# Sums of input tiles for the seven-product scheme, formed on the tensor engine in PSUM instead of on GpSimd

## Chip, cores and metric

The kernel runs on one core of one Trainium2 chip. The metric is the device time of one execution in microseconds. Three runs of the kernel before gave 1523.73, 1523.97 and 1529.43 us, a median of 1523.97 us.

## What is computed

One inference step of two trunk layers over 576 tokens, a prompt of 512 and eight samples of 8, with a model width of 1024. Layer 0 mixes time with RWKV-7 and retention heads side by side, layer 1 with a gated short convolution; a squared-ReLU MLP with 4096 hidden channels follows each mixer, and each step ends in a LayerNorm over the residual. Everything is fp32.

```python
def conv_mixer(x, buf0, w_in, conv_w, w_out):
    bg, cg, h = jnp.split(x @ w_in, 3, axis=-1)
    u = cg * h
    ext = jnp.concatenate([buf0.astype(u.dtype), u], axis=1)
    conv = sum(ext[:, j:j + T] * conv_w[j] for j in range(CONV_W))
    return (bg * conv) @ w_out, ext[:, ext.shape[1] - (CONV_W - 1):]

def sqrelu_mlp(x, w_up, w_down):
    return jnp.square(jax.nn.relu(x @ w_up)) @ w_down
...
        x = layer_norm(ALPHA * x + y, ln1_g[l], ln1_b[l])
        x = layer_norm(ALPHA * x + sqrelu_mlp(x, w_up[l], w_down[l]), ln2_g[l], ln2_b[l])
```

## The kernel before

The first stage, some 480 us, is the mixer of layer 0 and is not touched. The rest, `trunk` from line 1692 on, holds the MLP of layer 0, the convolution layer and the MLP of layer 1.

**Layout.** The activations stand transposed, channels on the 128 partitions and the 576 tokens along the free dimension, as eight tiles `x[0..7]`. Each is worked on in two halves of 288 tokens, g = 0 and g = 1. To keep fp32 accuracy, each operand of a matmul is split in two parts of type fp32r, a high part (the value rounded, a copy on ACT) and a low part (the value less its high part, a subtraction on DVE). `parts` (lines 72 to 79) makes them; in a profile their tiles are named h or l with a letter: wh and wl for weights, he and le, ho and lo for the input, hh and hl for the hidden tiles, ht and lt for the sums below. A product of two split operands is three matmuls (`mm3`, line 150): high by high, high by low, low by high.

**Weights.** Weight tiles of 128 x 1024 come by DMA into raw buffers, and `ensure` splits them ahead of their use (lines 77 and 78). Units in the set `T.pairs` are loaded two at a time, and `prepare` (line 117) forms their sums and differences on POOL and DVE (the helper of line 123).

**Two kinds of product.** `gemm` (line 157) does a plain product: for each output tile and half, 8 k-steps of three matmuls into one of six accumulators acc. `gemm7` (line 185) and `chained7` (line 225) do two output tiles and both halves with seven products of half the depth instead of eight, by Strassen's scheme in Winograd's form: the input is taken as a 2 x 2 block matrix, with even and odd tiles `x[2k]` and `x[2k+1]` and the two halves as its blocks. Three of the seven products take blocks as they are: el, the even tile's first half (`xe`), and both halves ol and or of the odd tile (`xo`). The other four take sums of blocks: er - el, or - (er - el), or - er, and ol - (or - (er - el)), which are kept split in `xt[k]`, n = 0 to 3. `x7` (line 1790) lists what each of the seven products takes: el, ol, then sums 1, 0 and 2, then or, then sum 3.

**Where the sums are formed.** `sums` (line 1720) forms 4 x 4 sums. For each k, four subtractions on GpSimd (POOL in the profile) go from the fp32 tiles x to two wide tiles ts, and then two calls of `split` go from ts to xt. It is called as `after` of three plain products, by line 181: in the MLP of layer 0, whose first product (unit 38) has four plain tiles, after the four tiles' first halves; in the convolution (unit 102, six plain tiles, three of them the head) and in the MLP of layer 1 (unit 134, four plain tiles), after both halves of the head. The second half of the even tiles, er, is stored split in the two upper hidden tiles (`b12`, line 1713).

**LayerNorm.** The last tiles of the product ahead end in `ln0_finish`, `ln_finish` and `ln_end`. They write the input's parts (lines 344, 345, 375, 376), and after them the fp32 tile x (lines 346 and 377), which is the residual. Their sums over channels are matmuls into PSUM tiles cps, ps and pq, from the pool `misc` of two banks (line 1663).

**Order.** Each engine has one queue. The program is built under `TileContext(nc, schedule_with_timeline_sim=True)`, which fixes each engine's order when it is built: among the instructions that an estimated timeline has ready, the one that was written first goes first. So products can be mixed in PE's queue.

The choices that bear on this: `NPL = 4` plain tiles, `SUMV = ()` (none of the sums on DVE), `FAR1, FAR2 = 3, 4` weight tiles of the next product split ahead into the tiles of xt, and these lines:

```python
x7 += [xe, [cut(a, gs[0]) for a in xo]] + [[(a[0][:, n], a[1][:, n]) for a in xt] for n in (1, 0, 2)] + [[cut(a, gs[1]) for a in xo], [(a[0][:, 3], a[1][:, 3]) for a in xt]]
T.gemm(102, 6, xs, evac_in, head=3, after=sums)
```

Of the kernel before, what the change touches and what calls it, by code (L numbers as in the profile page):

```python
# [10 lines left out]
F32 = mybir.dt.float32  # L11
F32R = mybir.dt.float32r
AF = mybir.ActivationFunctionType
ALU = mybir.AluOpType
PSUM = bass.MemoryType.PSUM

P = 128
NT = 576
GN = 288
# [476 lines left out]
def par_off():  # L496
    off, c = {}, 0
    for n, w in PARS:
        off[n] = (c, w)
        c += w  # L500
    return off, c
# [887 lines left out]
SUMV = ()  # L1389
# [114 lines left out]
def build(tc, i, o, coff):  # L1504
    nc = tc.nc
    T = Trunk(tc, i['w'], ahead=2)
    with ExitStack() as es:
        sr, sq = es.enter_context(ExitStack()), ExitStack()

        def pool(n, b, st=es, **k):  # L1510
            return st.enter_context(tc.tile_pool(name=n, bufs=b, **k))
# [5 lines left out]
        with ExitStack() as s1:  # L1517
            M = Mixers(T, i, o, coff)
# [28 lines left out]
            ts = [(M, M1)[k // 4].lr.rearrange('p a b c d -> p (a b c d)')[:, NT * (k % 4):NT * (k % 4 + 1)] for k in range(KT)]  # L1547
# [3 lines left out]
            for k, t in enumerate(ts):  # L1551
                x = nc.scalar.copy(M.xs[k][0], t)
# [106 lines left out]
        with ExitStack() as s2:  # L1659
            T.halves = False  # L1660
            T.cap = 2 * T.nu - 1
            wsp = [pool('wspa', WA, s2)] * WA
            T.pools([pool('raw3', RB, s2)], wsp, pool('acc', 6, s2, space=PSUM), pool('misc', 2, s2, space=PSUM), pool('tmp', 1, s2))
            T.start_at(38)
            T.tb = TB
            T.gated = GATED
            T.chunk, T.kfirst = CH, KF
            T.cfg = CFG
            T.pairs = {u + j for u in (38, 134) for j in range(NPL, 8, 2)} | {u + 16 * q + 2 * j for u in (38, 134) for q in range(1, 4) for j in range(4)} | set(range(108, 126, 2))
            hp = pool('hp', 1, s2)  # L1670
            T.ones1024 = hp.tile([P, P], F32, name='o1'); T.ones128 = hp.tile([P, P], F32, name='o2')
            T.eps = hp.tile([P, 1], F32, name='ep'); nc.gpsimd.memset(T.eps, LN_EPS)
            nc.gpsimd.memset(T.ones1024, 1 / 1024); nc.gpsimd.memset(T.ones128, 1 / 128)
            pre = nc.scalar.preload_act_table_set('natural_log_exp_and_others')
            for a in M.tabled:
                tc.add_manual_dep(pre.ins, a.ins.name, mybir.DependencyInfo(mybir.DependencyClass.NoSync, mybir.DependencyReason.DATA), reason='act table')
            T.pre = pre
            two = lambda n, w, hp=hp: tuple(hp.tile([P] + w, F32R, name=c + n) for c in ('h', 'l'))
            T.xe = [two(f'e{k}', [GN]) for k in range(4)]
            T.xo = [two(f'o{k}', [NT]) for k in range(4)]  # L1680
            T.hs = [(hp.tile([P, NT], F32R, name=f'hh{k}'), hp.tile([P, NT], F32R, name=f'hl{k}')) for k in range(KT)]
            nc.scalar.copy(T.hs[7][0], W.y[7])
            nc.vector.tensor_tensor(out=T.hs[7][1], in0=W.y[7], in1=T.hs[7][0].bitcast(F32), op=ALU.subtract)

            def opened():
                sq.close()
                T.p_w4 = xt = pool('xt', 1, s2)
                T.xt = [two(f't{k}', [4, GN], xt) for k in range(4)]
                if WB: wsp.extend([pool('wspb', WB, s2)] * WB)
            trunk(T, s2, par, i, o, W, opened)  # L1690

def trunk(T, es, par, i, o, W, opened):
    nc, tc, x, hs = T.nc, T.tc, T.x, T.hs
    xe, xo, xt = T.xe, T.xo, []
    pt = T.p_tmp
    po, _ = par_off()
# [4 lines left out]
    gs = [slice(0, GN), slice(GN, NT)]  # L1701
    b3 = lambda a: a.rearrange('p (b t) -> p b t', b=8)
    tmp = lambda n: pt.tile([P, GN], F32, tag='t', name=n, bufs=T.tb)
    cut = lambda pair, s: (pair[0][:, s], pair[1][:, s])
# [5 lines left out]
    def split(dst, src):  # L1710
        T.parts(*dst, src)

    def b12(k):
        return cut(hs[6 + k // 2], gs[k % 2])
# [3 lines left out]
        return cut(xo[k], gs[g]) if m % 2 else b12(k) if g else xe[k]  # L1718

    def sums():  # L1720
        for k in range(4):
            ts = [T.wide('ts').rearrange('p (a b) -> p a b', a=2) for _ in range(2)]
            t = lambda n: ts[n // 2][:, n % 2]
            (el, er), (ol, or_) = [[x[2 * k + j][:, s] for s in gs] for j in range(2)]
            for n, (a, b) in enumerate(((er, el), (or_, t(0)), (or_, er), (ol, t(1)))):
                (nc.vector if n in SUMV else nc.gpsimd).tensor_tensor(out=t(n), in0=a, in1=b, op=ALU.subtract)  # L1726
            for n in range(2): split((xt[k][0][:, 2 * n:2 * n + 2], xt[k][1][:, 2 * n:2 * n + 2]), ts[n])

    def xs(k, g):
        return cut(xo[k // 2], gs[g]) if k % 2 else b12(k // 2) if g else xe[k // 2]  # L1730
# [36 lines left out]
    def mlp(u, ln, out):  # L1767
        for q in range(4):
            n = NPL if q == 0 else 0
            if n: T.gemm(u, n, xs, evac_up, head=4, after=sums)  # L1770
            for j in range(n, 8, 2):
                T.gemm7(u + 16 * q + j, x7, evac_up7(j))
            T.gemm(u + 16 * q + 8, 8, hx, res_evac(T.ln_state(ln, x), lnpar(ln), out, first=q == 0, final=q == 3), tail=TL if q == 3 else 0, far=(FAR1 if ln == 1 else 0) if q == 3 else 0)
# [3 lines left out]
    for g in range(2):  # L1777
        for m, (hi, lo) in enumerate(W.w7):
            a = T.p_acc.tile([P, GN], F32, tag='acc', name='acc')
# [58 lines left out]
    def evac_in7(k0, w):  # L1838
        def f(j, t, a):
# [14 lines left out]
            else:  # L1854
# [4 lines left out]
                split(hs[k], t)  # L1859
        return f  # L1860
    T.gemm(102, 6, xs, evac_in, head=3, after=sums)
    for k in range(2, 8, 2):
        for w in range(3):
# [15 lines left out]
```

## Time and profile before

| | us |
|---|---|
| median of three runs | 1523.97 |
| the profiled execution | 1531.27 |
| its span, first to last instruction | 1529.3 |

The mean granted clock of PE over the span is 0.975. Busy times of a page are sums of durations within one engine. Matmuls are pipelined: the duration of one is longer than the distance between the starts of two, so PE's load is better read from how many matmuls stand in a stretch. The page's slices show PE full nearly throughout:

```profile
PE   8999999999998999999999999999998999999996
PEld 7999898989886989999999989999998999999996
DVE  4656766766857984845748679688799475574755
ACT  5343323333323851523515445444376253351533
POOL 1133213346533421311213547332543131121354
```

```profile
L152 PE MATMUL acc<-hh,wh 128*128 128x288 f32 x1180 | 345.9, 297 | 0.3 <-ACT hh L77 0.3
L152 PE MATMUL acc<-ht,wh 128*128 128x288 f32 x444 | 132.9, 300 | 13.7 <-ACT s L244 5.1
L152 PE MATMUL acc<-lt,wh 128*128 128x288 f32 x444 | 132.0, 298 | 3.8 <-DVE lt L78 3.8
```

A row of the groups reads: line, engine, operation, output <- inputs, shape, count; busy time and the mean of one in ns; idle time of the engine just before the group, and what ended most of it. The second and third row are products that take sums.

### The profile page before, as it was taken

What the parts mean: (1) busy time and instruction counts of PE and PEld (TensorE: products, weight loads), DVE (VectorE), ACT (ScalarE), POOL (GpSimd) and SP (SyncE); (2) the same over time, 40 slices, a digit from 0 to 9 for tenths busy, and PEclk for the clock granted to TensorE, in tenths of its full rate; (3) what the DMA queues carried; (4) which work ended last, traced back from release to release, by engine and by line L of the source; (5) the groups of instructions that cost most, each with busy time, mean ns of one, the idle gap of its engine ahead of it and who ended that gap; (6) DMA issues with size and microseconds to landing.
All of it is one profiled execution on the core that took longest, in us unless ns stands there. A gap on an engine that the chain in (4) does not pass through costs nothing. (4 is left out here: it accounts for less than half of the span.)

```text
span 1529.3 us, 29744 instructions
## 1 busy us (share of the span) xinstructions
PE 1473.3 (96%) x11792; PEld 1424.9 (93%) x11792; DVE 1046.1 (68%) x2019; ACT 646.8 (42%) x1365; POOL 499.5 (33%) x554
## 2 busy tenths in 40 slices
PE   8999999999998999999999999999998999999996
PEld 7999898989886989999999989999998999999996
DVE  4656766766857984845748679688799475574755
ACT  5343323333323851523515445444376253351533
POOL 1133213346533421311213547332543131121354
PEclk9999999999888999999999999999999999999998
DMA  5333334445312041331413402223303223142221
GB/s 182 107 88 89 88 100 135 143 123 172 96 43 106 2 136 57 98 97 57 136 57 98 132 7 69 80 87 121 103 1 125 70 87 107 56 126 68 86 67 63
DMA packets 71196, 140.04 MB, mean 92 GB/s; under 512 B 21488, under 2 KB 30944, under 8 KB 71056
## 3 DMA queue, kind: packets, MB, share of 16 engines
q1 hardware_dynamic: 68544, 130.87, 27.5%
q10 hardware_dynamic: 1440, 3.65, 0.7%
q0 software_dynamic: 1072, 3.61, 0.7%
q8 instruction: 93, 1.52, 0.4%
q14 instruction: 47, 0.39, 0.1%
HBM read 124.39 MB, written 13.70 MB: 90 GB/s over the span
## 5 line engine op out<-in xcount | busy, mean ns | idle before, releaser
L77 ACT CAST wh<-raw 128x512 fp32r<-128x512 f32 x440 | 252.7, 618 | 404.1 <-PE acc L152 269.6
L78 DVE TENSOR_TENSOR wl<-raw,wh 128x512 fp32r<-128x512 f32 x440 | 322.3, 765 | 46.9 <-ACT wh L77 41.2
L152 PE MATMUL acc<-hh,wl 128*128 128x288 f32 x1180 | 348.5, 296 | 0.0
L152 PE MATMUL acc<-hl,wh 128*128 128x288 f32 x1180 | 347.9, 296 | 0.0
L152 PE MATMUL acc<-hh,wh 128*128 128x288 f32 x1180 | 345.9, 297 | 0.3 <-ACT hh L77 0.3
L152 PEld LDWEIGHTS acc<-hl,wh 128*128 128x128 f32 x1180 | 221.5, 188 | 0.5
L152 PEld LDWEIGHTS acc<-hh,wl 128*128 128x128 f32 x1180 | 221.4, 188 | 0.5
L152 PEld LDWEIGHTS acc<-hh,wh 128*128 128x128 f32 x1180 | 220.5, 188 | 0.9 <-ACT hh L77 0.5
L152 PE MATMUL acc<-ht,wh 128*128 128x288 f32 x444 | 132.9, 300 | 13.7 <-ACT s L244 5.1
L152 PE MATMUL acc<-xh,wh 128*128 128x288 f32 x464 | 143.0, 308 | 0.0
L123 POOL TENSOR_TENSOR s<-raw 128x512 f32<-128x512 f32 x37 | 53.2, 1437 | 273.4 <-DMA raw<-in_w 208.2
L152 PE MATMUL acc<-xh,wl 128*128 128x288 f32 x464 | 141.0, 304 | 0.0
L152 PE MATMUL acc<-xl,wh 128*128 128x288 f32 x464 | 140.9, 304 | 0.0
L152 PE MATMUL acc<-lt,wh 128*128 128x288 f32 x444 | 132.0, 298 | 3.8 <-DVE lt L78 3.8
L152 PE MATMUL acc<-ht,wl 128*128 128x288 f32 x444 | 131.3, 298 | 0.0
L123 POOL TENSOR_TENSOR raw<-raw 128x512 f32<-128x512 f32 x37 | 57.4, 1552 | 163.7 <-DVE raw L123 110.7
L152 PE MATMUL acc<-ho,wh 128*128 128x288 f32 x352 | 104.2, 296 | 0.0
L152 PE MATMUL acc<-lo,wh 128*128 128x288 f32 x352 | 104.1, 297 | 0.0
L152 PE MATMUL acc<-ho,wl 128*128 128x288 f32 x352 | 103.5, 297 | 0.0
L152 PEld LDWEIGHTS acc<-ht,wh 128*128 128x128 f32 x444 | 84.8, 191 | 15.5 <-ACT s L244 5.4
L152 PEld LDWEIGHTS acc<-xh,wh 128*128 128x128 f32 x464 | 88.1, 190 | 2.5 <-issue 0.2
L152 PEld LDWEIGHTS acc<-xl,wh 128*128 128x128 f32 x464 | 88.1, 190 | 2.1 <-issue 0.2
(526 smaller groups left out, 3460.9 us busy)
## 6 DMA issues: line engine op xcount, KB each, us to landing
raw<-in_w SPq DMA_DIRECT2D x160, 512.0 KB, 3.9
raw<-in_w SPq DMA_DIRECT2D x60, 256.0 KB, 2.8
la<-in_w SPq DMA_DIRECT2D x32, 128.0 KB, 2.7
A<-stg SPq DMA_DIRECT2D x9, 288.0 KB, 2.3
x<-in_x POOLq DMA_DIRECT2D x8, 288.0 KB, 6.2
out_y<-x SPq DMA_DIRECT2D x16, 144.0 KB, 2.8
kr<-A SPq DMA_DIRECT2D x6, 288.0 KB, 2.7
lr<-in_x ACTq DMA_DIRECT2D x4, 288.0 KB, 7.5
```

The costliest lines, as they stand in the source:

```text
L77: a = self.nc.scalar.copy(hi[:, s], src[:, s])
L78: b = self.nc.vector.tensor_tensor(out=lo[:, s], in0=src[:, s], in1=hi[:, s].bitcast(F32), op=ALU.subtract)
L123: tt = lambda e, o, x, y, op: e.tensor_tensor(out=o, in0=x, in1=y, op=op)
L152: mm = lambda w, x, a, b: self.nc.tensor.matmul(acc, lhsT=w, rhs=x, start=a, stop=b, skip_group_check=onto)
```

## The change

The sums are no longer formed from the fp32 tiles x on GpSimd. PE forms each in a PSUM tile tps of the pool misc: every term is multiplied by plus or minus the identity, its high part and its low part in turn, and all of a sum's matmuls accumulate in one bank. Sum 0 has 2 terms, sum 1 has 3, sum 2 has 2, and sum 3 has 4, so 4, 6, 4 and 8 matmuls; each sum is now formed from input blocks directly rather than from an earlier sum. ACT then copies the bank to the high part, and DVE subtracts that from the bank for the low part, one half tile at a time. Before, ACT and DVE did two sums in one instruction, from SBUF. The places of the call are the same, and so is what xt holds. The two unit matrices, of 512 bytes a partition each, are made on ACT when the stage opens. The wide tiles ts are no longer used.

```diff
@@ -1669,6 +1669,8 @@
             hp = pool('hp', 1, s2)
             T.ones1024 = hp.tile([P, P], F32, name='o1'); T.ones128 = hp.tile([P, P], F32, name='o2')
+            T.unit = [hp.tile([P, P], F32R, name=f'u{n}') for n in range(2)]
+            for n in range(2): nc.scalar.activation(T.unit[n], M.C['ident'], AF.Copy, scale=2.0 * n - 1.0)
             T.eps = hp.tile([P, 1], F32, name='ep'); nc.gpsimd.memset(T.eps, LN_EPS)
@@ -1718,13 +1720,18 @@
     def sums():
+
         for k in range(4):
-            ts = [T.wide('ts').rearrange('p (a b) -> p a b', a=2) for _ in range(2)]
-            t = lambda n: ts[n // 2][:, n % 2]
-            (el, er), (ol, or_) = [[x[2 * k + j][:, s] for s in gs] for j in range(2)]
-            for n, (a, b) in enumerate(((er, el), (or_, t(0)), (or_, er), (ol, t(1)))):
-                (nc.vector if n in SUMV else nc.gpsimd).tensor_tensor(out=t(n), in0=a, in1=b, op=ALU.subtract)
-            for n in range(2): split((xt[k][0][:, 2 * n:2 * n + 2], xt[k][1][:, 2 * n:2 * n + 2]), ts[n])
+            el, er = xe[k], b12(k)
+            ol, or_ = [cut(xo[k], s) for s in gs]
+            for n, terms in enumerate((((er, 1), (el, 0)), ((or_, 1), (er, 0), (el, 1)), ((or_, 1), (er, 0)), ((ol, 1), (or_, 0), (er, 1), (el, 0)))):
+                ps = T.p_misc.tile([P, GN], F32, tag='misc', name='tps')
+                mms = [(T.unit[sign], c) for x_, sign in terms for c in x_]
+                for i_, (w, c) in enumerate(mms):
+                    nc.tensor.matmul(ps, lhsT=w, rhs=c, start=i_ == 0, stop=i_ == len(mms) - 1)
+                hi, lo = [a[:, n] for a in xt[k]]
+                nc.scalar.copy(hi, ps)
+                nc.vector.tensor_tensor(out=lo, in0=ps, in1=hi.bitcast(F32), op=ALU.subtract)
```

## The prediction

> **What bounds the kernel now.** I read the page's busy line first, then the table of 20 us stretches around the three places where the sums are formed, then the waits of PE there.
>
> ```profile
> span 1529.3 us, 29744 instructions
> PE 1473.3 (96%) x11792; PEld 1424.9 (93%) x11792; DVE 1046.1 (68%) x2019; ACT 646.8 (42%) x1365; POOL 499.5 (33%) x554
> ```
>
> PE is busy for 96% of the span; 56.0 us of it (1529.3 - 1473.3) are idle. So anything given to PE is paid for in full unless it lands in idle time or makes idle time vanish. The sums are made after the first plain tiles of three products (lines 1770 and 1861): at about 519, 921 and 1136 us. The stretches there, with the matmul count behind PE's busy time:
>
> ```profile
> 520.00:540.00 20.00, 17.90 (x133) 17.43 (x131) 20.00 (x18) 17.33 (x40) 20.00 (x18) 1.00 0.16 53
> 540.00:560.00 20.00, 18.31 (x128) 18.31 (x129) 19.77 (x34) 10.90 (x21) 4.09 (x4) 0.91 0.41 123
> 560.00:580.00 20.00, 20.00 (x152) 20.00 (x152) 10.29 (x19) 6.50 (x12) 2.53 (x3) 1.00 0.37 116
> 900.00:920.00 20.00, 17.15 (x109) 15.70 (x108) 16.56 (x38) 11.77 (x28) 2.72 (x3) 0.92 0.01 2
> 920.00:940.00 20.00, 20.00 (x141) 20.00 (x140) 20.00 (x23) 10.94 (x24) 17.69 (x15) 0.91 0.23 79
> 940.00:960.00 20.00, 14.87 (x107) 14.63 (x106) 19.14 (x33) 10.51 (x22) 10.16 (x12) 0.94 0.18 56
> 960.00:980.00 20.00, 20.00 (x138) 0.89 0.30 97
> 1120.00:1140.00 20.00, 19.76 (x143) 19.16 (x142) 17.14 (x35) 13.80 (x33) 3.79 (x4) 1.00 0.01 1
> 1140.00:1160.00 20.00, 15.54 (x106) 15.31 (x105) 19.58 (x21) 13.06 (x28) 16.72 (x15) 0.91 0.15 49
> ```
>
> The columns are PE, PEld, DVE, ACT, POOL, then the granted clock (the 960:980 row is of PE alone). A saturated stretch holds 152 matmuls, so one 128x288 matmul takes 20.00/152 = **0.132 us** of PE's time; the durations near 0.30 us in the lists overlap. The missing ones count what PE loses: 19 + 24 matmuls at the first place (5.7 us), 45 + 14 at the second from 940 to 980 (7.8 us), 46 at the third (6.1 us), **19.6 us** together. What PE waits for there, one answer per place:
>
> ```profile
> PE acc L152 <- DVE lt L78: 3.8, 2, 2.5
> PE acc L152 <- ACT s L244: 5.1, 1, 5.1
> PE acc L152 <- ACT wh L77: 4.5, 1, 4.5
> ```
>
> The rest of the 19.6 us is a lower clock after each wait: matmuls then start 0.24 us apart (1152.58, 1152.82):
>
> ```profile
> 1152.58 0.44 PE L152 MATMUL acc<-lt,wh 128*128 128x288 f32 x1
> 1152.82 0.44 PE L152 MATMUL acc<-ht,vh 128*128 128x288 f32 x1
> ```
>
> Behind all three stands DVE, full from 520 to 560, 920 to 960 and 1140 to 1160, and POOL beside it. These rows of the timelines of DVE and of POOL show why:
>
> ```profile
> 518.89 0.51 DVE L345 SCALAR_TENSOR_TENSOR lo<-x,par,ho 128x288 fp32r<-128x288 f32 x1
> 519.32 1.07 DVE L345 SCALAR_TENSOR_TENSOR hl<-x,par,hh 128x288 fp32r<-128x288 f32 x1
> ...
> 897.22 0.44 DVE L293 TENSOR_TENSOR x<-x,acc 128x288 f32<-128x288 f32 x1
> ```
>
> ```profile
> 519.24 0.83 POOL L1726 TENSOR_TENSOR ts<-x 128x288 f32<-128x288 f32 x1 [27.75 <-ACT x L346]
> ...
> 894.13 3.82 POOL L406 TENSOR_TENSOR u<-u,ln 128x288 f32<-128x288 f32 x4 [0.46 <-DVE ln L398]
> ```
>
> One operation of one shape doubles, 0.51 to 1.07 us, as soon as POOL begins its sums; L293, which reads one operand from PSUM, takes 0.44 us while POOL works (894.13 + 3.82 = 897.95). So POOL's sums slow every DVE operation with two SBUF operands. At the third place the chain of work that ended last passes through the sums themselves:
>
> ```profile
> 1136.21 2.54 POOL ts L1726 x2
> ...
> 1143.91 5.81 POOL ts L1726 x5
> 1149.73 1.75 POOL raw L123
> 1151.50 2.18 ACT wh L77 x4
> ```
>
> The weight combination of line 123 sits in POOL's queue behind the sums, and PE's 4.5 us wait ends with it.
>
> **The change, part by part.** Removed, by the view of the tile ts:
>
> ```profile
> L1726 POOL TENSOR_TENSOR ts<-x,ts x24: 815/1253/1321, 521.0 to 1154.6; 128x288 f32<-128x288 f32 x24
> L77 ACT CAST ht<-ts x24: 657/674/680, 524.3 to 1156.2; 128x576 fp32r<-128x576 f32 x24
> L78 DVE TENSOR_TENSOR lt<-ts,ht x24: 742/1134/1848, 526.5 to 1159.3; 128x576 fp32r<-128x576 f32 x24
> L1726 POOL TENSOR_TENSOR ts<-x x12: 834/1190/2152, 519.2 to 1146.2; 128x288 f32<-128x288 f32 x12
> L1726 POOL TENSOR_TENSOR ts<-x,x x12: 1005/1027/1312, 520.0 to 1148.7; 128x288 f32<-128x288 f32 x12
> ```
>
> That is 48 POOL subtractions (by the medians 24 x 1.25 + 12 x 1.19 + 12 x 1.03 = 57 us), 24 casts on ACT (16.2 us) and 24 subtractions on DVE (27 us). No DMA is moved.
>
> Added on PE: for each k, four sums of 2, 3, 2 and 4 terms with two parts each, 4 + 6 + 4 + 8 = 22 matmuls; with 4 k and 3 places 264. The form is there before, a scaled identity as weights on a split tile of 288 columns, and so are the two evacuations from PSUM:
>
> ```profile
> L1780 PE MATMUL acc<-mhi,neg x16: 292/298/606, 486.6 to 502.0; 128*128 128x288 f32 x16
> L1464 ACT CAST mhi<-mx x2: 388/393/398, 483.9 to 484.2; 128x288 fp32r<-128x288 f32 x2
> L1465 DVE TENSOR_TENSOR mlo<-mx,mhi x2: 448/450/451, 485.7 to 486.1; 128x288 fp32r<-128x288 f32 x2
> L1453 ACT ACTIVATE neg<-cst x1: 309/309/309, 354.1 to 354.1; 128x128 fp32r<-128x128 f32 x1
> ```
>
> Its 0.298 us equals the other matmuls' duration, so it streams at 0.132 us: 264 x 0.132 = **34.7 us** on the bounding engine, 11.6 us per place. ACT gains 48 x 0.39 = 18.9 us for the 16.2 it loses, DVE 48 x 0.45 = 21.6 for 27: near even, on engines with room once the contention is gone (DVE is at 10.29 of 20 from 560 on). The two unit tiles are 2 x 0.31 us on ACT before the stage starts; I cost them at nothing, 0.6 us if ACT were late there.
>
> Gained back: at most the 19.6 us. First place: the four tiles' second halves (96 matmuls) and the 88 of the sums give PE 24 us of work before the products that wait for lt, and DVE is twice as quick; I take all 5.7. Third place: POOL's queue ahead of line 123 is empty and 11.6 us of PE work stand in the wait; all 6.1. Second place: the 5.1 us end with an ACT copy behind evacuations of the convolution, of which only DVE's lateness is cured; between 0 and 7.8 I take half, 3.9. Sum 15.7 us.
>
> New wait: each sum fills one of two banks and goes on when ACT and DVE have emptied it, and behind that matmul stands all of PE. A bank is free (0.30 - 0.13) + 0.39 + 0.45 = 1.0 us after its last matmul. The sums take 0.53, 0.79, 0.53 and 1.05 us, 2.90 for a k; the bank with the longer two needs 2 x 1.0 + 0.79 + 1.05 = 3.84. That is 0.94 us lost per k, 11.3 us over twelve, if nothing stands between; nothing at all if other matmuls do. The order already mixes products by readiness:
>
> ```profile
> 544.83 0.29 PE L152 MATMUL acc<-ho,wh 128*128 128x288 f32 x1
> 545.09 0.29 PE L152 MATMUL acc<-ht,wh 128*128 128x288 f32 x1
> 545.23 0.29 PE L152 MATMUL acc<-ho,wl 128*128 128x288 f32 x1
> ```
>
> At the first two places 96 and 144 matmuls of plain tiles can go between; at the third little but two products of twelve. I take 2 us. Sum: 34.7 - 15.7 + 2 = **+21 us**. Against the profiled execution's 1531.27 us (span 1529.3) that is 1552; the median of the runs is 1523.97, 7.3 us lower, and the forecast for a median is **1545 us**.
>
> **Rivals.** *The two banks become the bound.* ACT's and DVE's queues are in order and hold weight splits; if the emptying stands behind them, the 11.3 us are paid, and the recovery is perhaps a third (6): 34.7 - 6 + 11.3 = +40, 1564 us. For it: 16.56 to 20.00 us of DVE work per 20 us there; against it: that load is inflated by POOL.
>
> *The banks also cost the clock.* If PE pauses so often that the clock stays low through the sums, 264 matmuls go at 0.24 us: 28.5 us more than the +40, 1592 us. Against it: the granted clock fell only where PE stood idle for microseconds. The Trainium skill, "TensorE: Matmul & The Clock Gate", section "A second HAM failure mode: psum-queue depth-cycling", describes a kernel that cycled through PSUM banks and whose short pauses made the clock swing between half and full; by it this rival would be the outcome, and no row here shows pauses of that kind.
>
> *Not slower.* All idle time of PE around the three places is covered: beside the 19.6 us the missing matmuls of 900 to 940 (43 + 11) and of 1120 to 1140 (9), 8.3 us. Then 34.7 - 27.9 = +6.8, 1531 us, within 0.5%. It decides at 27.1 us recovered. For it: operands in parts are ready before the fp32 x that POOL waited for. Against it: the idle time from 900 to 920 ends with the very LayerNorm output that each sum needs, so no sum can run in it.
>
> **How the numbers follow.** Forecast (1536 to 1555) 0.72, banks 0.14, banks with clock 0.05, not slower 0.09. About 0.5% (7.6 us) is what a measurement of this kernel can tell from no change. The low end takes the whole recovery, 34.7 - 19.6 = +15, and 3 us for the spread between runs: 1536. The high end takes in the bank rival: 1566. Outside are the clock rival, no slowdown, and the edges, about 0.2. Faster 0.02, same 0.07, slower 0.91.
>
> **What would show it.** PE should have 12056 matmuls, POOL 506 instructions, DVE's L345 and L376 all near 0.51 us, and the stretches at the three places near 152 matmuls, with the waits for lt and for wh gone. The pace of the new matmuls is the test of the rivals: starts 0.13 us apart, or mixed with acc, is the forecast; gaps of 0.3 to 0.6 us ahead of a new group that end with a DVE subtraction are the banks; starts 0.24 us apart the clock. I am wrong if the waits stay although POOL is idle, or if one new matmul costs PE something other than 0.132 us.

## The result, and the profile after

The changed kernel takes 1541.86 us (median of four runs, 1539.95 to 1546.72), the kernel before 1526.49 us (four runs, 1523.73 to 1529.43). The ratio is 1.0101 with a 95% interval of 1.007 to 1.0132: **15.4 us slower**, where 21 were forecast and 1536 to 1566 us was the range.

The busy line of the profile after:

```profile
span 1538.0 us, 30258 instructions
PE 1493.7 (97%) x12056; PEld 1446.9 (94%) x12056; DVE 1017.9 (66%) x2043; ACT 650.4 (42%) x1391; POOL 442.8 (29%) x506
```

PE has 12056 matmuls and POOL 506 instructions, as worked out: 264 more and 48 fewer. The stretches at the three places, with the columns of before:

```profile
520.00:540.00 20.00, 20.00 (x152) 20.00 (x151) 13.78 (x26) 14.68 (x36) 2.67 (x2) 1.00 0.27 80
540.00:560.00 20.00, 20.00 (x153) 20.00 (x153) 11.71 (x23) 9.06 (x20) 2.34 (x2) 1.00 0.20 63
920.00:940.00 20.00, 19.55 (x135) 19.37 (x135) 16.22 (x35) 12.96 (x30) 3.43 (x4) 0.91 0.34 106
940.00:960.00 20.00, 20.00 (x153) 20.00 (x152) 12.71 (x27) 8.32 (x19) 3.90 (x4) 1.00 0.09 27
960.00:980.00 20.00, 20.00 (x153) 20.00 (x153) 10.43 (x19) 10.06 (x22) 2.59 (x2) 1.00 0.18 53
1140.00:1160.00 20.00, 20.00 (x153) 20.00 (x152) 17.84 (x31) 15.05 (x37) 3.87 (x3) 1.00 0.19 57
```

From 520 to 560, 940 to 980 and 1140 to 1160, PE holds 152 or 153 matmuls in each 20 us; before, these stretches held 106 to 138. DVE has fallen from a full 20.00 to 13.78 at the first place although it has 24 instructions more in all. The reason stands in the operations that write the low parts after the LayerNorm, line 345 at the first place and line 376 at the other two. Before (view of line 376):

```profile
L376 DVE SCALAR_TENSOR_TENSOR lo<-x,par,ho x8: 514/1064/1542, 918.1 to 1141.0; 128x288 fp32r<-128x288 f32 x8
```

After (views of the two lines):

```profile
L345 DVE SCALAR_TENSOR_TENSOR lo<-x,par,ho x8: 506/508/510, 503.6 to 517.0; 128x288 fp32r<-128x288 f32 x8
L376 DVE SCALAR_TENSOR_TENSOR lo<-x,par,ho x8: 504/512/514, 920.5 to 1143.0; 128x288 fp32r<-128x288 f32 x8
```

The three numbers are the shortest, the median and the longest in ns: the longest is 514 after and was 1542 before. The new instructions, in the view of the tile tps:

```profile
L1731 PE MATMUL tps<-hh,u x48: 292/297/298, 516.1 to 1171.2; 128*128 128x288 f32 x48
...
L1733 ACT CAST ht<-tps x48: 377/399/403, 517.5 to 1171.9; 128x288 fp32r<-128x288 f32 x48
L1734 DVE TENSOR_TENSOR lt<-tps,ht x48: 442/456/458, 518.4 to 1172.5; 128x288 fp32r<-128x288 f32 x48
```

They cost what the nearest rows of before had said (0.30, 0.39 and 0.45 us). PE's timeline shows them among the plain products without a pause, 0.13 us from start to start:

```profile
528.09 0.30 PE L152 MATMUL acc<-hh,wl 128*128 128x288 f32 x1
528.23 0.29 PE L1731 MATMUL tps<-hh,u 128*128 128x288 f32 x1
528.36 0.29 PE L1731 MATMUL tps<-hl,u 128*128 128x288 f32 x1
...
529.42 0.30 PE L1731 MATMUL tps<-le,u 128*128 128x288 f32 x1
529.55 0.30 PE L152 MATMUL acc<-ho,wh 128*128 128x288 f32 x1
```

**Where the time went, place by place.** Two fixed points of the order stand around each place: the first matmul with neg, at the head of the stage, and the LayerNorm matmuls cps of the product that follows. The last two times of a row are the first and last start. Before (view of the tile neg, then of the tile cps in three windows):

```profile
L1780 PEld LDWEIGHTS acc<-mhi,neg x16: 187/190/330, 486.6 to 501.9; 128*128 128x128 f32 x16
```

```profile
L282 PE MATMUL cps<-x,o x4: 404/405/406, 858.5 to 859.3; 128*128 128x288 f32 x4
L282 PE MATMUL cps<-x,o x4: 405/406/406, 1075.1 to 1076.0; 128*128 128x288 f32 x4
L282 PE MATMUL cps<-x,o x4: 404/405/406, 1471.3 to 1472.2; 128*128 128x288 f32 x4
```

After:

```profile
L1787 PEld LDWEIGHTS acc<-mhi,neg x16: 187/192/329, 481.6 to 498.2; 128*128 128x128 f32 x16
```

```profile
L282 PE MATMUL cps<-x,o x4: 404/405/406, 860.8 to 861.7; 128*128 128x288 f32 x4
L282 PE MATMUL cps<-x,o x4: 404/405/406, 1080.3 to 1081.2; 128*128 128x288 f32 x4
L282 PE MATMUL cps<-x,o x4: 404/405/406, 1480.0 to 1480.9; 128*128 128x288 f32 x4
```

The three distances are 371.9, 216.6 and 396.2 us before and 379.2, 219.5 and 399.7 us after: **+7.3, +2.9 and +3.5 us**, together +13.7, for 11.6 us of added matmuls at each place. So 4.3, 8.7 and 8.1 us came back, **21.1 us**, and the price of 34.7 was larger. The two spans differ by only 8.7 us since the mixer stage ahead, which the change doesn't touch, ended 5.0 us earlier in this profile; the distance from the first point to the last leaves that out, and it is used below (984.7 us before, 998.4 after).

### The profile page after: what moved, and what is told of

Read it like the earlier page. It is cut to its first block, busy times and chain, and to the rows that moved or that the text cites. A ratio compares the mean times of both kernels' runs of the same rounds, so it can differ in the third digit from the quotient of the medians.

```text
span 1538.0 us, 30258 instructions
## 1 busy us (share of the span) xinstructions
PE 1493.7 (97%) x12056; PEld 1446.9 (94%) x12056; DVE 1017.9 (66%) x2043; ACT 650.4 (42%) x1391; POOL 442.8 (29%) x506
## 5 line engine op out<-in xcount | busy, mean ns | idle before, releaser
L78 DVE TENSOR_TENSOR wl<-raw,wh 128x512 fp32r<-128x512 f32 x440 | 314.0, 747 | 49.8 <-ACT wh L77 43.8
L152 PEld LDWEIGHTS acc<-xh,wl 128*128 128x128 f32 x464 | 87.6, 189 | 1.6 <-issue 0.2
```

Source lines behind the costliest of these rows:

```text
L78: b = self.nc.vector.tensor_tensor(out=lo[:, s], in0=src[:, s], in1=hi[:, s].bitcast(F32), op=ALU.subtract)
L152: mm = lambda w, x, a, b: self.nc.tensor.matmul(acc, lhsT=w, rhs=x, start=a, stop=b, skip_group_check=onto)
```

## The experiments

**Theory A**: an added matmul costs 0.132 us of the span in full, and what came back are waits that POOL's sums had caused. **Rival B**: the waits would be there without POOL's sums, and vanish only because the other engines gain time while PE works on the sums. Beside these stood the rival of the two banks.

**The sums on DVE.**

```diff
-SUMV = ()
+SUMV = (0, 1, 2, 3)
```

> The kernel before with SUMV = (0, 1, 2, 3): the 48 subtractions run on DVE instead of POOL, nothing is added on PE. Theory A (POOL's sums made PE wait, by slowing DVE and by standing ahead of POOL's weight sums): 48 x 0.45 us = 21.6 us of DVE work are added, but DVE's other operations go back from 1.06 to 0.51 us; the waits at the three places mostly vanish, 8 to 20 us faster than before, ratio 0.987 to 0.995. Rival B (DVE is full there whatever POOL does, and the waits vanished only because 34.7 us of added PE work gave DVE time): the added DVE work lengthens PE's waits, same as before or up to 1% slower.

Measured: 1510.78 us against 1525.22 of before, ratio 0.9902 (0.9877 to 0.9928). It is faster than both kernels. DVE does the sums in 48 x 0.45 = 22 us where POOL took 57; the view of the tile ts:

```profile
L1726 DVE TENSOR_TENSOR ts<-x,ts x24: 445/450/1547, 518.2 to 1131.4; 128x288 f32<-128x288 f32 x24
```

Its three distances are 366.8, 208.0 and 394.8 us, 5.1, 8.6 and 1.4 less than before. At the third place a wait for a cast of the sums (ht) is left:

```profile
PE acc L152 <- ACT ht L77: 2.7, 1, 2.7
```

Rival B, by which 21.6 us of DVE work more would lengthen the waits, falls.

**No sums at all.**

```diff
-            ts = [T.wide('ts').rearrange('p (a b) -> p a b', a=2) for _ in range(2)]
...
-            for n in range(2): split((xt[k][0][:, 2 * n:2 * n + 2], xt[k][1][:, 2 * n:2 * n + 2]), ts[n])
+            for n in range(2): split((xt[k][0][:, 2 * n:2 * n + 2], xt[k][1][:, 2 * n:2 * n + 2]), x[2 * k + n].rearrange('p (a b) -> p a b', a=2))
```

> The kernel before without the sums: the parts of xt are split straight from the tiles x (blocks in place of the sums), so ACT and DVE do the same casts and subtractions as before and POOL's 48 and PE's 264 instructions are both left out. This is the gain alone. Theory A: the 19 to 21 us that the matmul counts of the traces show as recovered come back without any PE work: about 1506 us, ratio 0.987. Rival B (the waits are covered by PE's added work, not removed): within 5 us of before, ratio 0.997 to 1.0.

Measured: 1505.96 us, ratio 0.9862 (0.9836 to 0.9887). The distances:

```profile
L1775 PEld LDWEIGHTS acc<-mhi,neg x16: 187/189/330, 482.5 to 497.6; 128*128 128x128 f32 x16
```

```profile
L282 PE MATMUL cps<-x,o x4: 404/405/406, 848.5 to 849.3; 128*128 128x288 f32 x4
L282 PE MATMUL cps<-x,o x4: 405/406/406, 1056.4 to 1057.2; 128*128 128x288 f32 x4
L282 PE MATMUL cps<-x,o x4: 404/405/406, 1445.9 to 1446.8; 128*128 128x288 f32 x4
```

366.0, 207.9 and 389.5 us are 5.9, 8.7 and 6.7 less than before, 21.3 in all. In total the gain alone equals the 21.1 us that came back under the change; place by place the two differ by 1.6 us at most (5.9, 8.7 and 6.7 here, 4.3, 8.7 and 8.1 there). So the waits can go without any work on PE to cover them, and B falls here too.

**Each matmul of the sums twice.**

```diff
-            for n in range(2): nc.scalar.activation(T.unit[n], M.C['ident'], AF.Copy, scale=2.0 * n - 1.0)
+            for n in range(2): nc.scalar.activation(T.unit[n], M.C['ident'], AF.Copy, scale=n - 0.5)
...
-                mms = [(T.unit[sign], c) for x_, sign in terms for c in x_]
+                mms = [(T.unit[sign], c) for x_, sign in terms for c in x_ for _ in range(2)]
```

> The changed kernel with each matmul of the sums issued twice, with plus and minus one half on the diagonal, so 528 in place of 264 and the same result. Theory A (an added matmul costs 0.132 us of the span in full): 264 x 0.132 = 34.7 us more than the changed kernel, ratio to before about 1.033. Rival (the sums still fall partly into idle time, or cost more through the two banks): clearly less than 30 or more than 40 us more.

Measured: 1577.73 us, ratio 1.0344 (1.0316 to 1.0372). First point to last takes 1033.5 us (484.9 to 1518.4), 35.1 more than the changed kernel's 998.4, for 264 matmuls: 0.133 us each. The price of the term is measured by itself.

**Six banks in place of two.**

```diff
-                ps = T.p_misc.tile([P, GN], F32, tag='misc', name='tps')
+                ps = T.p_acc.tile([P, GN], F32, tag='acc', name='tps')
```

> The changed kernel with the sums formed in the six banks of acc instead of the two of misc. Theory A (other matmuls fill the time in which a bank is emptied): within 3 us of the changed kernel, ratio to before 1.008 to 1.012. Rival (two banks make PE wait): 5 to 11 us less than the changed kernel, ratio about 1.003 to 1.007.

Measured: 1541.4 us, ratio 1.0098 (1.0072 to 1.0124), the changed kernel's 1.0101 within the intervals. The two banks cost nothing; that rival falls, and with it the one by which their pauses would lower the clock.

**POOL's subtractions put back, for nobody.** What of POOL's sums made PE wait: that they slow DVE, that they hold POOL's queue, or that they are late themselves? This kernel is the one without sums, with the four removed subtractions for each k restored.

```diff
+            ts = [T.wide('ts').rearrange('p (a b) -> p a b', a=2) for _ in range(2)]
...
+            for n, (a, b) in enumerate(((er, el), (or_, t(0)), (or_, er), (ol, t(1)))):
+                nc.gpsimd.tensor_tensor(out=t(n), in0=a, in1=b, op=ALU.subtract)
             for n in range(2): split((xt[k][0][:, 2 * n:2 * n + 2], xt[k][1][:, 2 * n:2 * n + 2]), x[2 * k + n].rearrange('p (a b) -> p a b', a=2))
```

> The kernel without sums (parts of xt split straight from x, 1506 us) with POOL's 48 subtractions put back, their results read by nobody: the sums are left out of the products. Theory A1 (POOL's subtractions cost by being on POOL: they slow DVE's operations with two SBUF operands and hold up POOL's queue): DVE's L345 and L376 go back to about 1.06 us beside them and most of the 19 us return, 1515 to 1526 us, ratio 0.993 to 1.0. Rival A2 (only the chain POOL to ACT to DVE, the lateness of the sums themselves, cost): within 3 us of 1506, ratio 0.985 to 0.989.

Measured: 1530.6 us against 1527.55 of before, run beside it, ratio 1.0029 (1.001 to 1.0048). All of the gain is lost, a little more than the top of what A1 allowed, though no instruction waits for these results. First point to last takes 989.9 us (478.3 to 1468.2), 26.5 more than without them. DVE is slowed again, in the view of line 376:

```profile
L376 DVE SCALAR_TENSOR_TENSOR lo<-x,par,ho x8: 511/1060/1539, 909.5 to 1131.8; 128x288 fp32r<-128x288 f32 x8
```

And PE's old waits are back, at the second and the third place:

```profile
PE acc L152 <- ACT s L244: 6.0, 1, 6.0
...
PE acc L152 <- ACT wh L77: 6.3, 2, 4.5
```

So the loss doesn't need the lateness of the sums themselves (A2). Two causes are left, the slower DVE and POOL's queue, and at the third place the trace shows both. The 4.5 us wait there (in the 6.3) ends with a cast of a weight sum that POOL makes in line 123 from a tile that DVE writes. From the timelines of DVE and POOL, before and then in this kernel:

```profile
1141.99 1.29 DVE L123 TENSOR_TENSOR raw<-s,raw 128x512 f32<-128x512 f32 x1
1149.68 1.78 POOL L123 TENSOR_TENSOR raw<-raw 128x512 f32<-128x512 f32 x1
```

```profile
1132.80 1.29 DVE L123 TENSOR_TENSOR raw<-s,raw 128x512 f32<-128x512 f32 x1
1140.82 1.48 POOL L123 TENSOR_TENSOR raw<-raw 128x512 f32<-128x512 f32 x1
```

POOL begins 6.4 us after DVE's tile is there before (1149.68 less 1143.28) and 6.7 us after it here, and works on subtractions in between. Without sums it begins 0.1 us after it.

**POOL held by fills.**

```diff
...
+            ts = [T.wide('ts') for _ in range(2)]
+            for n in range(2):
+                nc.gpsimd.tensor_copy(ts[n][:, 0:1], x[2 * k + 1][:, NT - 1:NT])
+                for _ in range(4): nc.gpsimd.memset(ts[n], 0.0)
...
```

> The kernel without sums (1506 us) with POOL held by fills of constants in place of its subtractions: for each k two copies of one column of x and eight fills of 128x576, which read nothing from SBUF, an estimate of 4 us against 4.7 us of subtractions. Theory A1a (the slowdown of DVE by two readers is what costs): DVE's L345 and L376 stay near 0.51 us and the time within 5 us of 1506, ratio 0.985 to 0.990. Rival A1b (POOL's queue ahead of its weight sums is what costs): PE waits for weights as before the change, and 1513 to 1526 us, ratio 0.992 to 1.0, with DVE at 0.51 us.

Measured: 1503.38 us, ratio 0.9858 (0.9837 to 0.9878), the same as with POOL idle. The fills took more of POOL than the estimate (view of the tile ts):

```profile
L1725 POOL MEMSET ts<- x96: 572/578/594, 517.5 to 1138.8; 128x576 f32 x96
L1724 POOL COPY ts<-x x24: 183/456/3848, 513.6 to 1124.5; 128x1 f32<-128x1 f32 x24
```

96 x 0.578 + 24 x 0.456 (medians) = 66 us, more than the 57 of the subtractions, and POOL is full or nearly so at each place (the last busy time, ahead of the clock), while PE holds 149 to 153:

```profile
520.00:540.00 20.00, 20.00 (x153) 20.00 (x152) 13.96 (x24) 12.90 (x31) 20.00 (x37) 1.00 0.16 54
920.00:940.00 20.00, 20.00 (x153) 20.00 (x152) 17.07 (x31) 8.60 (x18) 18.86 (x34) 1.00 0.17 54
1120.00:1140.00 20.00, 19.64 (x149) 19.40 (x148) 17.26 (x27) 15.22 (x34) 19.36 (x34) 1.00 0.16 54
```

Line 376 takes at most 0.524 us here. In the stretches that follow, 540 to 560 and 940 to 960, PE holds 141 and 144, but the three distances together are those of the kernel without sums.

What this settles differs by place. POOL's weight sum of line 123 begins later after DVE's tile here than with the subtractions for nobody at the first place (5.0 us against 0.1) and at the second (4.0 against 1.9), yet the distances are 3.5 and 9.9 us shorter: there the queue is not the cause, and what is left is the slowdown of DVE. At the third place the fills hold it only half as long:

```profile
1117.99 0.69 DVE L123 TENSOR_TENSOR raw<-s,raw 128x512 f32<-128x512 f32 x1
1121.66 1.30 POOL L123 TENSOR_TENSOR raw<-raw 128x512 f32<-128x512 f32 x1
```

It begins 3.0 us after DVE's tile, not 6.7. So at the third place this kernel does not part the two causes.

**Fewer matmuls, from split sums.**

```diff
-            for n, terms in enumerate((((er, 1), (el, 0)), ((or_, 1), (er, 0), (el, 1)), ((or_, 1), (er, 0)), ((ol, 1), (or_, 0), (er, 1), (el, 0)))):
+            tt = [(xt[k][0][:, n], xt[k][1][:, n]) for n in range(4)]
+            for n, terms in enumerate((((er, 1), (el, 0)), ((or_, 1), (tt[0], 0)), ((or_, 1), (er, 0)), ((ol, 1), (tt[1], 0)))):
```

> The changed kernel with sum 1 formed as or less the split sum 0 and sum 3 as ol less the split sum 1, so 16 matmuls for a k in place of 22, 192 in all in place of 264. Theory A (each matmul costs 0.132 us): 72 x 0.132 = 9.5 us less than the changed kernel, ratio to before about 1.004. Rival (the dependent sums wait for ACT and DVE, with PE behind them): less than 5 us gained, ratio above 1.007.

Measured: 1532.05 us, ratio 1.0041 (1.0015 to 1.0066). First point to last takes 989.9 us (482.8 to 1472.7), 8.5 less than under the change; 72 x 0.132 = 9.5 were expected. PE's one wait for a cast of the sums at the three places is 0.6 us, so the rival's waits did not come.

**The sums on DVE in two passes.**

```diff
-SUMV = ()
+SUMV = (0, 1, 2, 3)
...
+        first = []
+        for k in range(4):
...
+            nc.vector.tensor_tensor(out=ts[:, 0], in0=er, in1=el, op=ALU.subtract)
+            nc.vector.tensor_tensor(out=ts[:, 1], in0=or_, in1=ts[:, 0], op=ALU.subtract)
+            split((xt[k][0][:, 0:2], xt[k][1][:, 0:2]), ts)
+            first.append(ts)
+        for k in range(4):
...
+            nc.vector.tensor_tensor(out=ts[:, 0], in0=or_, in1=er, op=ALU.subtract)
+            nc.vector.tensor_tensor(out=ts[:, 1], in0=ol, in1=first[k][:, 1], op=ALU.subtract)
+            split((xt[k][0][:, 2:4], xt[k][1][:, 2:4]), ts)
```

> The kernel with the sums on DVE, in two passes: sums 0 and 1 of all four k first, then 2 and 3, since the product that waits first takes sum 1 of every k. Theory (what is left of PE's waits with the sums on DVE, 2.7 us at the third place for a cast of the sums, is their order): 0 to 5 us less than the sums on DVE in one pass (ratio 0.990), so 0.987 to 0.990. Rival (the order is not what ends last): 0.990 or above.

Measured: 1515.28 us, ratio 0.9936 (0.9917 to 0.9956): no gain over the one pass (0.9902). First point to last takes 972.1 us against 969.6, so within the stage the two passes are 2.5 us slower, and PE's waits for casts of the sums at the third place are 3.7 us against 2.7. The theory about the order falls. The traces show what comes before those casts in ACT's queue. With the sums on DVE in one pass, from the timelines of POOL and ACT:

```profile
1117.84 5.87 POOL L123 TENSOR_TENSOR raw<-raw 128x512 f32<-128x512 f32 x1 [19.80 <-DVE raw L123]
1123.74 2.19 ACT L77 CAST wh<-raw 128x512 fp32r<-128x512 f32 x4 [4.42 <-POOL raw L123]
```

POOL's weight sum, 1.29 us at this place after the change, takes 5.87 us beside DVE's sums. ACT waits 4.42 us for it, and its first cast of a sum follows at 1126.91. In two passes the weight sum takes 5.82 us and ACT waits 6.01. So DVE's sums slow POOL in turn. That this chain is what makes PE wait is read from the traces; no run tried it.

First point to last, for all kernels:

| kernel | us | against before |
|---|---|---|
| before | 984.7 | |
| after | 998.4 | +13.7 |
| each matmul twice | 1033.5 | +48.8 |
| six banks | 1000.1 | +15.4 |
| from split sums | 989.9 | +5.2 |
| subtractions for nobody | 989.9 | +5.2 |
| sums on DVE, two passes | 972.1 | -12.6 |
| sums on DVE | 969.6 | -15.1 |
| POOL held by fills | 963.6 | -21.1 |
| no sums | 963.4 | -21.3 |

## Why the prediction was right

**The bound, and the price of 34.7 us**: right. Doubling the matmuls added 35.1 us, so PE had no room for them at any place.

**The cause of PE's waits**: right. DVE's operations with two SBUF operands double beside POOL's subtractions, and that made the weights and the sums' parts late. Subtractions that nobody reads bring the waits back, fills of POOL do not. The Trainium skill, "SBUF — State Buffer", section "Who interferes with whom", has the same rule: a DVE instruction with two SBUF inputs contends with a GpSimd instruction that reads SBUF, and not with one that only writes it. The runs agree with both halves of it: 1.06 us at the median beside subtractions (line 376, lo), at most 0.524 beside fills. The prediction read a second cause from the chain at the third place, POOL's queue ahead of line 123. It stands there in the traces, 6.4 us before and 6.7 with subtractions for nobody. How much of the loss at that place is the queue's and how much the slower DVE's stays open, since the fills held the queue for only 3.0 us.

**What came back, 15.7 us taken of at most 19.6**: too small, and here lies most of the difference between +21 and +13.7 in the stage. The first place gave 4.3 us (5.7 taken), the second 8.7 (3.9 taken), the third 8.1 (6.1 taken). The term that was mis-sized most is the second place. The evacuations that its wait ended with were late because of POOL's subtractions: PE waits 6.0 us for that ACT copy (line 244) with subtractions for nobody and 1.0 us with fills. All of it came back. The top of 19.6 us was itself 1.5 us too low. Where these came from is not shown: the stretch from 920 to 940, which the count left out, holds 135 matmuls after and held 141 before. The lower clock "after each wait", from which the prediction explained part of the count, holds after the waits of 2.47, 5.13 and 4.46 us; after one of 1.32 us (537.76) the starts stay 0.13 us apart.

**The new wait, 2 us taken of 0 to 11.3**: with six banks the time is the same, so it was nothing. The third place, where little seemed to stand between the sums, shows 153 matmuls in 20 us.

**The rivals**: none came. The banks cost nothing with two or with six, the clock stayed at 1.00 while the sums ran at the first and the third place (at the second it was 0.91 from 920 to 940, as before the change, and three of the new matmuls start 0.24 us apart, from 922.44), and a slowdown within 0.5% lies outside the interval (1.007 at its low end); for that 27.1 us would have had to come back, and 21 did. The median came closer to the forecast of 1545 us than the difference did, since the kernel before took 1526.49 us in these runs, 2.5 more than the median that the forecast started from; that part is luck.

**Evacuations and unit tiles at nothing**: right. DVE lost load at all three places, and no instruction of PE waited for the unit tiles.

## What to carry to other kernels

On a bound engine, an added instruction costs its issue distance (here 0.13 us, not the 0.30 of its row), and idle time beside it pays only if the reason for that idle time goes too. Before work is moved off an engine, ask what else its reads slow and what its queue holds up: here the gain of 21 us came without any work on PE, and moving the sums to DVE, the seemingly full engine, took 15 us of it without the bill of 34.7. An engine that is full because another one slows it has room once that one stops.

## What the runs showed of the hardware

The mixer stage, the same in all these kernels, ended between 478.3 and 486.6 us in the ten profiles (first matmul with neg). A difference of some us between two spans can come from there (5.0 us between before and after, where the spans differ by 8.7); a distance between two points of the changed stage leaves that out.

Subtractions on POOL that no one reads made the kernel slightly slower than when PE waits for their results (ratio 1.0029). At the third place PE then held 84 matmuls in 20 us at a clock of 0.74:

```profile
1140.00:1160.00 20.00, 15.07 (x84) 14.49 (x84) 17.45 (x23) 7.77 (x17) 11.96 (x10) 0.74 0.16 53
```

PE waits three times for weights there, 4.49, 0.97 and 1.79 us, where the kernel before waits once, 4.46 us. Why the second and third wait came was not tried.
